# Joining the first two of three attention groups early, and the third to them last, in a two-layer encoder

## The chip, the cores and the metric

The kernel runs on one core of a Trainium2 chip. The metric is device time in microseconds (us) of one execution; the kernel before takes 2418.27 us (median of 3 runs, 2415.06 to 2419.82).

## The reference

The program is a two-layer encoder over one sequence of 1024 tokens with 1024 features, all in float32. Layer 1 mixes tokens by windowed grouped-query attention, layer 2 by dilated attention; each is followed by a SwiGLU feed-forward. Layer 2 is the one changed. It runs three attention groups (8 query heads each, heads of 64) whose outputs are combined by a softmax over the groups' log-denominators:

```python
outs, lses = [], []
for gi, (window, dil) in enumerate(((128, 1), (512, 4), (2048, 16))):
    half = window // (2 * dil)
    o, lse = banded_attention(to_strided(q[:, :, gi], dil), to_strided(k[:, :, gi], dil),
                              to_strided(v[:, :, gi], dil), half, slopes[gi], dil)
    outs.append(from_strided(o, b, dil))
    lses.append(from_strided(lse, b, dil))
alpha = softmax(stack(lses), axis=0)              # over the three groups
o = einsum('nbshg,nbshgd->bshgd', alpha, stack(outs))
x = x + g1 * (o.reshape(b, s, 512) @ w_out)
h = rmsnorm(x) * (1 + sc2) + sh2
x = x + g2 * ((silu(h @ w_gate) * (h @ w_up)) @ w_ffn_out)
```

## The kernel before

**Number format.** A float32 product is made of three products in TensorE's faster float32 format, of a rounded part ("high") and a remainder ("low") of each factor: `acc3`, lines 283 to 285. So every weight and every activation is first split: a ScalarE copy gives the high part, a VectorE or GpSimd subtraction the low part (weights: L179 on ScalarE, L180 on GpSimd; the normalised input `h` of a feed-forward: L255 on VectorE, L256 and L258 on ScalarE, L261 on VectorE or L259 on GpSimd, as the table `LOWS` says for each of 8 row blocks).

**Layer 2's attention.** `layer_b` goes through 48 *units*: 16 of group 2, then for each half `t` of the tokens 8 of group 1 and 8 of group 0. A unit has two parts. `first` makes four blocks of scores (two TensorE products each, L489 and L490), takes their maxima on VectorE (L492) and their exponentials and sums on ScalarE (L502). `second`, two units later, transposes the probabilities (L531), splits them (L533 on ScalarE, L534 on VectorE), multiplies by the values (L525) and adds two halves (L546 on ScalarE, L547 on VectorE). The outputs of groups 1 and 2 go to DRAM (`od`), as they come in another order of tokens; those of group 0 stay in SBUF (`o1`). Maxima and denominators of groups 1 and 2 take a way through DRAM as well and come back, ordered by token, by `relay(t)`: a load `rl` (L1045), a copy (L1047), four transposes (L1050) and a copy into `st12` (L1051). Units 24 to 31 are group 0 of half 0, units 40 to 47 group 0 of half 1.

**The combination of a half.** `alphas(t)` makes the weights of all three groups at once (L1066 to L1086: small VectorE operations, two ScalarE activations, four transposes L1084, the rows `al_r` L1086). `out_load` fetches the outputs of groups 1 and 2. `combine(t, g, ...)`, for each of four head pairs g, spreads the weights of the three groups over 128 partitions (three products with a 0/1 matrix `sel`, L1111), multiplies the three outputs (L1116 and L1117 with a change of the order of tokens, L1119), adds them (L1120, L1121) and splits the sum (L1122 on ScalarE, L1123 on VectorE). For half 0 this stands at units 32 to 36; for half 1 it stands behind unit 47.

**What fills TensorE beside the units.** 201 *fill* steps are handed out among the units by a table of due numbers (`FILL_B`): 160 projections of queries and keys, 32 of the output projection of half 0 (`out_0`, with residual L353 and the sums for the norm), and 9 of `up_early`, the first feed-forward tile of half 0 (8 steps of six products and an empty one). By the table 200 are handed out by unit 48; a loop behind the units hands out what is left, which is the empty one. Then `up(f)` for tiles 1 and 2 follows.

**Order.** The program is written once and a scheduler of the tile framework places each instruction in its engine's queue; each engine then works in the order of its queue. PSUM tiles are shared by tags of two buffers each: `s` (scores), `t` (transposes), `o` (outputs), and the products' banks. In `combine` the spreads take tags `o` and `s`.

Of the kernel before, what the change touches and what calls it, by code (L numbers as in the profile page):

```python
# [57 lines left out]
def f32(ap):  # L58
    return ap.bitcast(F)
# [15 lines left out]
class Trunk:  # L75
# [791 lines left out]
    def layer_b(self, h, x_src):  # L867
        nc, a, sb = self.nc, self.a, self.sb
        layer = 1
        dram = self.dram  # L870
        vd = dram.tile([T, 3, 2, P], F, name="vd")
        qd = dram.tile([3, 4, 2, P, T], F, name="qd")
# [180 lines left out]
        def alphas(t):  # L1053


            us = slice(4 * t, 4 * t + 4)

            def by_unit(ap):
                return ap.rearrange("p (u k g) -> p u k g", u=4, k=2)

            m0, l0 = (stats[0][:, :, us, s].rearrange("p k u g -> p u k g") for s in range(2))
            m, l = (st12[:, s:4:2].rearrange("p x u h -> p x (u h)") for s in range(2))
            w, e = (wk.tile([P, 3, 32], F, name=n, tag=n, bufs=1) for n in ("al_w", "al_e"))
            top = wk.tile([P, 32], F, name="al_t", tag="al_t", bufs=1)
            v = nc.vector.tensor_tensor
            v(top, m[:, 0], m[:, 1], op=ALU.min)  # L1066
            v(by_unit(top), by_unit(top), m0, op=ALU.min)
            v(by_unit(w[:, 0]), by_unit(top), m0, op=ALU.subtract)
            v(w[:, 1:3], top.unsqueeze(1).broadcast_to([P, 2, 32]), m, op=ALU.subtract)
            nc.scalar.activation(w, w, AF.Exp)  # L1070
            v(by_unit(e[:, 0]), by_unit(w[:, 0]), l0, op=ALU.mult)
            v(e[:, 1:3], w[:, 1:3], l, op=ALU.mult)
            v(top, e[:, 0], e[:, 1], op=ALU.add)
            v(top, top, e[:, 2], op=ALU.add)
            nc.vector.reciprocal(top, top)
            v(w, w, top.unsqueeze(1).broadcast_to([P, 3, 32]), op=ALU.mult)
            fl = wk.tile([P, 4, 48], R, name="al_f", tag="al_f", bufs=1)
            fv = fl.rearrange("p u (x s h) -> p x u s h", x=3, s=2)
            wv = w.rearrange("p x (u h) -> p x u h", u=4)
            nc.scalar.activation(fv[:, :, :, 0], wv, AF.Copy)  # L1080
            v(fv[:, :, :, 1], wv, f32(fv[:, :, :, 0]), op=ALU.subtract)
            tp = psp.tile([P, HT], F, name="ps_t", tag="t", bufs=2)
            for u in range(4):
                nc.tensor.transpose(tp[0:48, u * P:(u + 1) * P], f32(fl[:, u]), self.ident)  # L1084
            rows = wk.tile([48, HT], R, name="al_r", tag="al_r", bufs=1)
            nc.scalar.activation(rows, tp[0:48], AF.Copy)  # L1086
            return rows

        def out_load(t, i):

            if t == 0:
                x = self.htile([2, 2, HT], F)
                got = [x[:, 0], x[:, 1]]
            else:
                got = [wk.tile([P, 2, HT], F, name="ol", tag=tag, bufs=n) for tag, n in ((("q2", 2), ("q2", 2)), (("v", 2), ("p", 3)))[i]]
            g = slice(2 * i, 2 * i + 2)
            nc.sync.dma_start(got[0], od[1][:, g].rearrange("p g (r i) -> p g r i", r=4)[:, :, :, t * P:(t + 1) * P].rearrange("p g r i -> p (g r) i"))
            nc.sync.dma_start(got[1], od[2][:, g, t])
            return got

        def combine(t, g, got, rows):

# [3 lines left out]
            o2, o3 = (x[:, g % 2] for x in got)
            al = []
            for gi in range(3):
                ps = psp.tile([P, HT], F, name="ps_al", tag="os"[gi > 0], bufs=2)
                c = (4 * gi + g) * P  # L1110
                nc.tensor.matmul(ps, lhsT=sel[:, c:c + P], rhs=rows, start=True, stop=True)  # L1111
                al.append(ps)
            s = al[0]
            w2, w3 = (wk.tile([P, HT], F, name=n, tag="t2", bufs=self.t2) for n in ("w2", "w3"))
            v = nc.vector.tensor_tensor
            v(w2.rearrange("p (i r) -> p r i", r=4), o2.rearrange("p (r i) -> p r i", r=4), al[1].rearrange("p (i r) -> p r i", r=4), op=ALU.mult)  # L1116
            v(w3.rearrange("p (i j r) -> p j r i", j=8, r=2), o3.rearrange("p (j r i) -> p j r i", r=2, i=32),  # L1117
              al[2].rearrange("p (i j r) -> p j r i", j=8, r=2), op=ALU.mult)
            v(s, o1[t][:, g], s, op=ALU.mult)  # L1119
            v(s, s, w2, op=ALU.add)  # L1120
            v(s, s, w3, op=ALU.add)  # L1121
            nc.scalar.activation(oT[0][:, g], s, AF.Copy)  # L1122
            v(oT[1][:, g], s, f32(oT[0][:, g]), op=ALU.subtract)  # L1123
# [10 lines left out]
        def out_0(d):  # L1134
# [9 lines left out]
            self.residual(spill["x"][d], ps, layer, 2, d)  # L1144
            self.square(spill["x"][d], d, spill["ssq"], wk)
# [15 lines left out]
        for i, (gi, kv, u) in enumerate(units):  # L1161
# [44 lines left out]
        for k in range(KT):  # L1206
            nc.sync.dma_start(self.xs[0][k], spill["x"][k])
# [87 lines left out]
def _arrays(np, i):  # L1295
# [15 lines left out]
    o["sel"] = np.kron(np.eye(3), np.kron(np.ones((2, 1)), np.kron(np.eye(8).reshape(8, 2, 4).transpose(0, 2, 1).reshape(8, 8), np.ones((1, 64))))).astype(np.float32)  # L1311
# [45 lines left out]
```

## Time and profile before

| | |
|---|---|
| median of 3 runs | 2418.27 us |
| the profiled execution | 2420.43 us, its span 2418.6 us |
| TensorE (PE) busy | 2277.5 us, 94% |
| VectorE (DVE) busy | 1286.0 us, 53% |
| ScalarE (ACT) busy | 883.4 us, 37% |
| GpSimd (POOL) busy | 732.6 us, 30% |
| mean granted TensorE clock | 0.970 of 2.4 GHz |

The span is the time from the first to the last instruction of the profiled execution. Busy shares are means over stages that differ much: in the 183 us from 1480 to 1663, which hold the units from the end of half 0's group 0 to the last, TensorE is busy for 159.53, VectorE for 146.44, ScalarE for 115.62 and GpSimd for 52.14 us.

### The profile page before, as it was taken

To read this page: it belongs to the slowest core of one execution; us is meant where nothing else is said; L and a number is where in the kernel's file an instruction comes from. 1 tells how busy PE (TensorE), PEld (TensorE's weight loads), DVE (VectorE), ACT (ScalarE), POOL (GpSimd) and SP (SyncE) were. 2 spreads that over 40 slices of the span, in tenths; PEclk is the share of its full clock that TensorE was granted. 3 is DMA by queue.
4 is the path that set the end of the run, shared out by engine and by line. 5 is a ranking of instruction groups with operands and counts; after the bars stand their busy time and mean duration, and the time that the engine had idled before them with its cause. 6 is when DMAs were issued, how large, how long until landed. Compare 5 with 4: busy or idle time off the path is not lost. (4 is left out here: it accounts for less than half of the span.)

```text
span 2418.6 us, 28059 instructions
## 1 busy us (share of the span) xinstructions
PE 2277.5 (94%) x10520; PEld 1867.3 (77%) x10520; DVE 1286.0 (53%) x2263; ACT 883.4 (37%) x1754; POOL 732.6 (30%) x471
## 2 busy tenths in 40 slices
PE   6799898989999999999989999988999999999997
PEld 5587777767788888888879878665788888888886
DVE  8869999578533333333361568874633332222325
ACT  4549887232111111111252788662411111111111
POOL 4525443443122122222132344332432212221210
PEclk9899998989999999999999999987999999999998
DMA  7431123666411111111234766433221111111101
GB/s 281 157 134 36 40 92 122 217 200 220 155 60 39 49 44 53 44 53 45 82 129 156 196 188 194 152 102 111 90 79 53 44 53 53 53 50 47 53 18 70
DMA packets 128281, 242.62 MB, mean 100 GB/s; under 512 B 37632, under 2 KB 65024, under 8 KB 127120
## 3 DMA queue, kind: packets, MB, share of 16 engines
q1 hardware_dynamic: 128144, 240.82, 31.1%
q8 instruction: 83, 1.36, 0.2%
q14 instruction: 54, 0.44, 0.1%
HBM read 208.14 MB, written 30.54 MB: 99 GB/s over the span
## 5 line engine op out<-in xcount | busy, mean ns | idle before, releaser
L283 PE MATMUL ps_d<-h,w 128*128 128x512 f32 x1968 | 781.4, 399 | 16.7 <-ACT h L256 6.5
L284 PE MATMUL ps_d<-h,w 128*128 128x512 f32 x1968 | 778.2, 396 | 8.7 <-DVE h L261 7.1
L285 PE MATMUL ps_d<-h,w 128*128 128x512 f32 x1968 | 775.7, 395 | 3.5 <-POOL w L180 3.5
L180 POOL TENSOR_TENSOR w<-raw,w 128x1024 fp32r<-128x1024 f32 (+1 forms) x178 | 429.5, 2415 | 815.6 <-ACT w L179 797.9
L283 PEld LDWEIGHTS ps_d<-h,w 128*128 128x128 f32 x1968 | 375.2, 191 | 91.5 <-ACT w L179 8.6
L285 PEld LDWEIGHTS ps_d<-h,w 128*128 128x128 f32 x1968 | 375.1, 191 | 85.2 <-POOL w L180 6.0
L284 PEld LDWEIGHTS ps_d<-h,w 128*128 128x128 f32 x1968 | 376.1, 191 | 81.6 <-DVE h L261 10.2
L400 DVE TENSOR_TENSOR u<-silu,ps_d 128x512 f32<-128x512 f32 x88 | 60.4, 686 | 623.0 <-PE ps_d L285 607.1
L353 DVE SCALAR_TENSOR_TENSOR x<-ps_d,mod,x 128x512 f32<-128x512 f32 x368 | 270.3, 747 | 148.4 <-PE ps_d L285 148.2
L179 ACT ACTIVATE w<-raw 128x1024 fp32r<-128x1024 f32 (+1 forms) x178 | 185.6, 1046 | 359.6 <-PE ps_d L285 288.7
L283 PE MATMUL ps_d<-act,wo 128*128 128x512 f32 x704 | 275.9, 392 | 8.0 <-DVE x L353 4.5
L285 PE MATMUL ps_d<-act,wo 128*128 128x512 f32 x704 | 274.6, 390 | 0.0
L284 PE MATMUL ps_d<-act,wo 128*128 128x512 f32 x704 | 274.6, 390 | 0.0
L180 POOL TENSOR_TENSOR wo<-raw,wo 128x1024 fp32r<-128x1024 f32 x44 | 105.6, 2400 | 434.7 <-ACT wo L179 434.7
L179 ACT ACTIVATE wo<-raw 128x1024 fp32r<-128x1024 f32 x44 | 46.6, 1060 | 384.8 <-PE ps_d L285 340.6
L283 PEld LDWEIGHTS ps_d<-act,wo 128*128 128x128 f32 x704 | 132.5, 188 | 38.3 <-DVE x L353 6.3
L285 PEld LDWEIGHTS ps_d<-act,wo 128*128 128x128 f32 x704 | 132.5, 188 | 27.8
L284 PEld LDWEIGHTS ps_d<-act,wo 128*128 128x128 f32 x704 | 132.6, 188 | 27.0
L402 DVE TENSOR_TENSOR act<-u,act 128x512 fp32r<-128x512 f32 x88 | 126.5, 1437 | 49.0 <-ACT act L401 48.9
L152 DVE SCALAR_TENSOR_TENSOR ada_acc<-ada_w,cond,ada_acc 128x1024 f32<-128x1024 f32 x70 | 115.8, 1655 | 49.1 <-DMA ada_w<-in_ada_w 48.4
L401 ACT ACTIVATE act<-u 128x512 fp32r<-128x512 f32 x88 | 55.0, 625 | 215.1 <-DVE u L400 215.0
L534 DVE TENSOR_TENSOR pp<-ps_t,pp 128x512 fp32r<-128x512 f32 x168 | 114.9, 685 | 12.0 <-ACT pp L533 10.1
(176 smaller groups left out, 2651.9 us busy)
## 6 DMA issues: line engine op xcount, KB each, us to landing
raw<-in_ffn_w_in SPq DMA_DIRECT2D x102, 512.0 KB
ada_w<-in_ada_w SPq DMA_DIRECT2D x80, 512.0 KB
raw<-in_ffn_w_out SPq DMA_DIRECT2D x44, 512.0 KB
raw<-in_b_w_q SPq DMA_DIRECT2D x24, 512.0 KB
qd<-qo SPq DMA_DIRECT2D x48, 256.0 KB
h<-in_ada_w SPq DMA_DIRECT2D x8, 1024.0 KB
raw<-in_a_w_out SPq DMA_DIRECT2D x16, 512.0 KB
q<-qd SPq DMA_DIRECT2D x16, 512.0 KB
```

The lines of the kernel that those rows point to most:

```text
L152: nc.vector.scalar_tensor_tensor(acc, w, s, acc, op0=ALU.mult, op1=ALU.add)
L179: self.nc.scalar.activation(w[:, 0], raw, AF.Copy)
L180: self.nc.gpsimd.tensor_tensor(w[:, 1], raw, f32(w[:, 0]), op=ALU.subtract)
L283: mm(ps, lhsT=w[0], rhs=x[0], start=first, stop=False)
L284: mm(ps, lhsT=w[0], rhs=x[1], start=False, stop=False)
L285: mm(ps, lhsT=w[1], rhs=x[0], start=False, stop=last)
L353: self.nc.vector.scalar_tensor_tensor(x, ps, self.mod[:, layer, c * 8 + d:c * 8 + d + 1], x, op0=ALU.mult, op1=ALU.add)
L400: nc.vector.tensor_tensor(u, s, up, op=ALU.mult)
L401: nc.scalar.activation(act[:, 0, halves(t)], u, AF.Copy)
L402: nc.vector.tensor_tensor(act[:, 1, halves(t)], u, f32(act[:, 0, halves(t)]), op=ALU.subtract)
L534: nc.vector.tensor_tensor(pp[n, 1], tp[n], f32(pp[n, 0]), op=ALU.subtract)
```

## The change

The combination is split in two. `weights_12` makes a softmax over groups 1 and 2 alone and keeps their joint maximum and denominator (`ml12`); `join_12` weighs these two outputs and adds them in place (`o2`). `weights` makes a softmax over two terms, group 0 and the joint one, and `join` weighs and adds these. `weights_12` stands at units 29 (half 0) and 44 (half 1), `join_12` at units 30 and 31, and 45 and 46, for two head pairs each; `weights` and `join` stand where `alphas` and `combine` stood. `relay` of half 1 goes from unit 44 to 43, and the loads of the outputs follow it for both halves. The spreads of `join_12` take the tag `s`, which the scores use. Half 0's residual is written to DRAM (`x_mid`, 8 writes of 256 KB) when it is made, and loaded from there for the rest of the feed-forward, not copied from SBUF. The loop over the fill steps left goes behind the last join.

```diff
+        def weights_12():
+            m, l = (st12[:, s:4:2].rearrange("p x u h -> p x (u h)") for s in range(2))
+            w, e = small()
+            tt(ml12[:, 0], m[:, 0], m[:, 1], op=ALU.min)
+            tt(w, ml12[:, 0:1].broadcast_to([P, 2, 32]), m, op=ALU.subtract)
+            nc.scalar.activation(w, w, AF.Exp)
+            tt(e, w, l, op=ALU.mult)
+            tt(ml12[:, 1], e[:, 0], e[:, 1], op=ALU.add)
+            return rows_of(w)
+
+        def weights(t):
...
+            tt(by_unit(top), by_unit(ml12[:, 0]), m0, op=ALU.min)
...
+            nc.vector.reciprocal(top, top)
+            tt(w, w, top.unsqueeze(1).broadcast_to([P, 2, 32]), op=ALU.mult)
+            return rows_of(w)
...
+        def spread(x, g, rows, tag):
+            ps = psp.tile([P, HT], F, name="ps_al", tag=tag, bufs=2)
+            c = (4 * x + g) * P
+            nc.tensor.matmul(ps, lhsT=sel[:, c:c + P], rhs=rows, start=True, stop=True)
+            return ps
+
+        def join_12(g, x, rows):
+            o2, o3 = x[:, 0, g % 2], x[:, 1, g % 2]
+            a1, a2 = (spread(i, g, rows, "s") for i in range(2))
+            w2 = wk.tile([P, HT], F, name="w2", tag="t2", bufs=self.t2)
+            tt(w2.rearrange("p (i r) -> p r i", r=4), o2.rearrange("p (r i) -> p r i", r=4), a1.rearrange("p (i r) -> p r i", r=4), op=ALU.mult)
+            a3 = a2.rearrange("p (i j r) -> p j r i", j=8, r=2)
+            tt(a3, o3.rearrange("p (j r i) -> p j r i", r=2, i=32), a3, op=ALU.mult)
+            tt(o2, a2, w2, op=ALU.add)
+
+        def join(t, g, x, rows):
...
+            s, a12 = (spread(i, g, rows, "os"[i]) for i in range(2))
+            w2 = wk.tile([P, HT], F, name="w2", tag="t2", bufs=self.t2)
+            tt(w2, x[:, 0, g % 2], a12, op=ALU.mult)
+            tt(s, o1[t][:, g], s, op=ALU.mult)
+            tt(s, s, w2, op=ALU.add)
             nc.scalar.activation(oT[0][:, g], s, AF.Copy)
-            v(oT[1][:, g], s, f32(oT[0][:, g]), op=ALU.subtract)
+            tt(oT[1][:, g], s, f32(oT[0][:, g]), op=ALU.subtract)
...
             self.residual(spill["x"][d], ps, layer, 2, d)
+            nc.sync.dma_start(x_mid[d], spill["x"][d])
...
-            elif i in (28, 44):
+            elif i in (28, 43):
                 relay(i // 40)
-                if i == 28:
-                    got = [out_load(0, j) for j in range(2)]
+                got = [out_load(i // 40, j) for j in range(2)]
+            elif i in (29, 44):
+                rows = weights_12()
+            elif i in (30, 31, 45, 46):
+                for g in (0, 1) if i in (30, 45) else (2, 3):
+                    join_12(g, got[g // 2], rows)
             elif i == 32:
-                rows = alphas(0)
+                rows = weights(0)
             elif 33 <= i <= 36:
-                combine(0, i - 33, got[(i - 33) // 2], rows)
+                join(0, i - 33, got[(i - 33) // 2], rows)
                 if i == 36:
                     self.most = 1000
-        while self.fill:
-            self.fill_step()
-        rows = alphas(1)
-        got = [out_load(1, i) for i in range(2)]
+        rows = weights(1)
         while pend:
             run(second(*pend.popleft()))
         for g in range(4):
-            combine(1, g, got[g // 2], rows)
+            join(1, g, got[g // 2], rows)
+        while self.fill:
+            self.fill_step()
...
         for k in range(KT):
-            nc.sync.dma_start(self.xs[0][k], spill["x"][k])
+            nc.sync.dma_start(self.xs[0][k], x_mid[k])
```

Three places in the engines' queues. The first is TensorE's queue in half 0, at the end of unit 31 (group 0's last unit of that half; `q2` are its queries, `ps_s` its scores, `ps_d` a fill product, `ps_o` a weighing). Before:

```order
L525 MATMUL ps_o_12028<-pp_12034,v_11810 128x512
L489 MATMUL ps_s_12073<-kh_11107,q2_11960 128x256
L490 MATMUL ps_s_12073<-kl_11109,q2_11960 128x256
L283 MATMUL ps_d_12042<-h_9218,w_12043 128x512
L284 MATMUL ps_d_12042<-h_9218,w_12043 128x512
L285 MATMUL ps_d_12042<-h_9218,w_12043 128x512
L525 MATMUL ps_o_12028<-pp_12034,v_11810 128x512
L531 MATMUL ps_t_12105<-cst_66,p_11972 128x128 x4
L489 MATMUL ps_s_12115<-kh_9939,q2_12090 128x192
L490 MATMUL ps_s_12115<-kl_9941,q2_12090 128x192
```

Now, at the same place:

```order
L490 MATMUL ps_s_12105<-kl_11108,q2_11976 128x256
L283 MATMUL ps_d_12074<-h_9218,w_12075 128x512
L284 MATMUL ps_d_12074<-h_9218,w_12075 128x512
L285 MATMUL ps_d_12074<-h_9218,w_12075 128x512
L525 MATMUL ps_o_12152<-pp_12172,v_11809 128x512 x2
L1116 MATMUL ps_al_12122<-al_r_11974,sel_9285 128x512
L1116 MATMUL ps_al_12124<-al_r_11974,sel_9285 128x512
L1116 MATMUL ps_al_12130<-al_r_11974,sel_9285 128x512
L1116 MATMUL ps_al_12132<-al_r_11974,sel_9285 128x512
L489 MATMUL ps_s_12163<-kh_9938,q2_12138 128x192
L490 MATMUL ps_s_12163<-kl_9940,q2_12138 128x192
L489 MATMUL ps_s_12178<-kh_9938,q2_12138 128x192
```

Four spreads of `join_12` (`ps_al`) stand in a row between the last unit of group 0 and the first scores of the next unit, where a fill product and a transpose stood. The second place is VectorE's queue at the end of the units of half 1. Before, from the first split of unit 45's probabilities to the weights' last small operation but one:

```order
L534 TENSOR_TENSOR pp_13342<-ps_t_13337,pp_13342 128x512
L1068 TENSOR_TENSOR al_w_13387<-al_t_13389,stat0_9295 128x32
L1069 TENSOR_TENSOR al_w_13387<-al_t_13389,st12_9294 128x64
L547 TENSOR_TENSOR o1_1_9938<-ps_o_13285,os_13284 64x4x128
L534 TENSOR_TENSOR pp_13356<-ps_t_13351,pp_13356 128x512
L1071 TENSOR_TENSOR al_e_13388<-al_w_13387,stat0_9295 128x32
L1072 TENSOR_TENSOR al_e_13388<-al_w_13387,st12_9294 128x64
L1073 TENSOR_TENSOR al_t_13389<-al_e_13388 128x32
L1074 TENSOR_TENSOR al_t_13389<-al_t_13389,al_e_13388 128x32
L1075 RECIPROCAL al_t_13389<-al_t_13389 128x32
L547 TENSOR_TENSOR o1_1_9938<-ps_o_13336,os_13335 64x4x128
L1076 TENSOR_TENSOR al_w_13387<-al_w_13387,al_t_13389 128x96
```

Now, from unit 46's last maxima to the first of unit 47 (`h_13197` holds the loaded outputs of groups 1 and 2):

```order
L492 ISA stat0_9294 128x1
L492 ISA p_13367,stat0_9294<-ps_s_13394,bias_13208 128x256
L492 ISA stat0_9294 128x1
L1124 TENSOR_TENSOR w2_13412<-h_13197,ps_al_13408 128x4x128
L1126 TENSOR_TENSOR ps_al_13410<-h_13197,ps_al_13410 128x16x32
L547 TENSOR_TENSOR o1_1_9937<-ps_o_13425,os_13424 64x4x128
L1124 TENSOR_TENSOR w2_13420<-h_13197,ps_al_13416 128x4x128
L1127 TENSOR_TENSOR h_13197<-ps_al_13410,w2_13412 128x512
L1126 TENSOR_TENSOR ps_al_13418<-h_13197,ps_al_13418 128x16x32
L1127 TENSOR_TENSOR h_13197<-ps_al_13418,w2_13420 128x512
L492 ISA p_13434,stat0_9294<-ps_s_13436,bias_13202 128x192
L492 ISA stat0_9294 128x1
```

The weights of all groups stood there; now it is the second half of `join_12`, and unit 47's maxima are queued behind it. The third place is ScalarE's queue where the feed-forward begins. Before (`h_13467` is the combined output, `w_13595` the second weight of tile 1):

```order
L1122 ACTIVATE h_13467<-ps_al_13484 128x512
L398 ACT_TABLE_LOAD
L398 ACTIVATE silu_13576<-ps_d_12997 128x512
L1122 ACTIVATE h_13467<-ps_al_13499 128x512
L179 ACTIVATE w_13595<-raw_13596 128x1024
L401 ACTIVATE act_13575<-u_13578 128x512
L1122 ACTIVATE h_13467<-ps_al_13514 128x512
```

Now (`w_13654` is that weight):

```order
L1139 ACTIVATE h_13546<-ps_al_13558 128x512
L398 ACT_TABLE_LOAD
L398 ACTIVATE silu_13635<-ps_d_13031 128x512
L1139 ACTIVATE h_13546<-ps_al_13568 128x512
L401 ACTIVATE act_13634<-u_13637 128x512
L1139 ACTIVATE h_13546<-ps_al_13578 128x512
L179 ACTIVATE w_13654<-raw_13655 128x1024
```

The copy of the second weight stood ahead of the fourth head pair's split (L1122); now it stands behind the fourth (L1139).

## Rows read from the trace of the kernel before

**Rows 1.** Engines by stretch: busy us, instructions, TensorE clock; columns in the first line.

```profile
core 0: us, PE busy (x) PEld busy (x) DVE busy (x) ACT busy (x) POOL busy (x), PEclk, DMA share, GB/s
1480.00:1515.00 35.00, 32.20 (x183) 25.84 (x181) 28.88 (x83) 28.85 (x78) 11.89 (x10) 1.00 0.67 222
1515.00:1548.00 33.00, 30.60 (x141) 21.34 (x140) 31.52 (x67) 20.49 (x51) 10.83 (x12) 0.95 0.50 157
...
1606.00:1615.00 9.00, 9.00 (x44) 7.31 (x42) 1.12 (x4) 3.47 (x10) 2.57 (x2) 0.87 0.25 66
1615.00:1628.40 13.40, 9.26 (x52) 6.74 (x51) 10.79 (x36) 10.30 (x29) 2.71 (x2) 1.00 0.60 173
1628.40:1642.80 14.40, 13.05 (x34) 7.24 (x34) 6.89 (x9) 4.16 (x7) 0.00 (x0) 0.51 0.15 59
1642.80:1658.30 15.50, 7.57 (x12) 3.07 (x12) 15.25 (x22) 5.75 (x8) 2.35 (x1) 0.50 0.23 87
1658.30:1663.00 4.70, 4.70 (x11) 3.72 (x12) 1.07 (x2) 0.00 (x0) 0.00 (x0) 0.51 0.85 267
```

**Rows 2.** Timeline by engine: start, us, operation, [idle before it <-what ended it].

```profile
1589.39 1.08 PE L243 MATMUL ps_d<-cst,st 128*128 128x128 f32 x8
...
1603.19 2.52 POOL L259 TENSOR_TENSOR h<-ht,h 128x512 fp32r<-128x512 f32 x2 [7.67 <-ACT ht L258]
...
1609.21 1.28 POOL L259 TENSOR_TENSOR h<-ht,h 128x512 fp32r<-128x512 f32 x1 [0.93 <-ACT ht L258]
...
1614.19 0.43 PE L1050 MATMUL ps_t<-cst,rp 32*128 32x32 f32 x4
...
1614.66 0.40 ACT L1051 ACTIVATE st<-ps_t 128x128 f32<-128x128 f32 x1 [5.53 <-PE ps_t L1050]
...
1615.09 0.19 DVE L1066 TENSOR_TENSOR al_t<-st 128x32 f32<-128x32 f32 x1 [6.10 <-ACT st L1051]
```

**Rows 3.** Timeline from the weights of half 1 to the feed-forward's first tile.

```profile
1627.94 0.26 DVE L1081 TENSOR_TENSOR al_f<-al_w,al_f 128x96 fp32r<-128x96 f32 x1 [0.35 <-ACT al_f L1080]
...
1628.81 2.00 PE L531 MATMUL ps_t<-cst,p 128*128 128x128 f32 x8
...
1642.11 0.68 DVE L547 TENSOR_TENSOR o<-ps_o,os 64x512 f32<-64x512 f32 x1 [3.91 <-ACT os L546]
...
1642.83 0.69 DVE L1119 TENSOR_TENSOR ps_al<-o,ps_al 128x512 f32<-128x512 f32 x1
...
1647.28 1.70 PE L1111 MATMUL ps_al<-al_r,sel 48*128 48x512 f32 x2 [3.64 <-DVE w L1117]
...
1654.74 1.05 ACT L179 ACTIVATE w<-raw 128x1024 fp32r<-128x1024 f32 x1
...
1655.84 0.79 PE L283 MATMUL ps_d<-h,w 128*128 128x512 f32 x1 [1.73 <-ACT w L179]
...
1658.27 0.80 PE L285 MATMUL ps_d<-h,w 128*128 128x512 f32 x1 [1.22 <-POOL w L180]
```

**Rows 4.** VectorE's operations by form, 1480 to 1660 us: count, busy, mean ns, idle.

```profile
L534 DVE TENSOR_TENSOR pp<-ps_t,pp 128x512 fp32r<-128x512 f32 x45 | 30.8, 686 | 6.1 <-ACT pp L533 5.5
L492 DVE CUSTOM_DVE_ANT_0 p<-ps_s,bias 128x256 f32<-128x256 f32 x36 | 14.7, 420 | 4.0 <-PE ps_s L490 3.5 <-PE ps_t L531 0.3
...
L547 DVE TENSOR_TENSOR o<-ps_o,os 64x512 f32<-64x512 f32 x16 | 11.0, 688 | 6.8 <-ACT os L546 6.1
...
L1121 DVE TENSOR_TENSOR ps_al<-ps_al,w 128x512 f32<-128x512 f32 x8 | 5.6, 698 | 0.0
...
L1116 DVE TENSOR_TENSOR w<-ol,ps_al 128x512 f32<-128x512 f32 x4 | 4.3, 1073 | 1.3 <-PE ps_al L1111 1.3
...
L1117 DVE TENSOR_TENSOR w<-ol,ps_al 128x512 f32<-128x512 f32 x4 | 4.1, 1013 | 0.0
```

**Rows 5.** SyncE's loads near the end of the units, start and time to landing.

```profile
1605.73 0.80 SPq L1045 DMA_DIRECT2D rl<-sd  x2
...
1626.10 31.26 SPq L1207 DMA_DIRECT2D x<-h  x8
```

More of the change, by code (lines that the diff above doesn't have):

```diff
@@ L871, in layer_b @@
         vd = dram.tile([T, 3, 2, P], F, name="vd")
+        x_mid = dram.tile([KT, P, HT], F, name="x_mid_b")
         qd = dram.tile([3, 4, 2, P, T], F, name="qd")
@@ L881, in layer_b @@
         self.raw = deque([(self.main, 1), (kp, 1)])
-        sel = kp.tile([48, 12 * P], R, name="sel")
-        for i in range(3):
-            raw = kp.tile([48, HT], F, name="sel_f", tag="qo", bufs=3)
+        tt = nc.vector.tensor_tensor
+        sel = kp.tile([32, 8 * P], R, name="sel")
+        for i in range(2):
+            raw = kp.tile([32, HT], F, name="sel_f", tag="qo", bufs=3)
             nc.sync.dma_start(raw, a["sel"][:, i * HT:(i + 1) * HT])
@@ L887, in layer_b @@
         st12 = kp.tile([P, 4, 4, 8], F, name="st12")
+        ml12 = kp.tile([P, 2, 32], F, name="ml12")
         stats = [kp.tile([P, 2, 8, 2, 4], F, name=f"stat{i}") for i in range(3)]
@@ L1051, in relay @@
             nc.scalar.activation(st12.rearrange("p x u h -> p x h u"), tp.rearrange("p (x h u) -> p x h u", x=4, h=8), AF.Copy)
[L1053 to L1078, printed above, removed]
@@ L1079, in alphas, with by_unit, small, rows_of @@
+        def by_unit(ap):
+            return ap.rearrange("p (u k g) -> p u k g", u=4, k=2)
+        def small():
+            return (wk.tile([P, 2, 32], F, name=n, tag=n, bufs=1) for n in ("al_w", "al_e"))
+        def rows_of(w):
+            fl = wk.tile([P, 4, 32], R, name="al_f", tag="al_f", bufs=1)
+            fv = fl.rearrange("p u (x s h) -> p x u s h", x=2, s=2)
             wv = w.rearrange("p x (u h) -> p x u h", u=4)
             nc.scalar.activation(fv[:, :, :, 0], wv, AF.Copy)
-            v(fv[:, :, :, 1], wv, f32(fv[:, :, :, 0]), op=ALU.subtract)
+            tt(fv[:, :, :, 1], wv, f32(fv[:, :, :, 0]), op=ALU.subtract)
@@ L1101, in combine @@
-        def combine(t, g, got, rows):
+                nc.tensor.transpose(tp[0:32, u * P:(u + 1) * P], f32(fl[:, u]), self.ident)
+            rows = wk.tile([32, HT], R, name="al_r", tag="al_r", bufs=2)
+            nc.scalar.activation(rows, tp[0:32], AF.Copy)
+            return rows
+        def weights_12():
[7 more added lines that the diff above has]
+            return rows_of(w)
@@ new lines, in weights @@
+        def weights(t):
+            m0, l0 = (stats[0][:, :, 4 * t:4 * t + 4, s].rearrange("p k u g -> p u k g") for s in range(2))
+            w, e = small()
+            top = wk.tile([P, 32], F, name="al_t", tag="al_t", bufs=1)
+            tt(by_unit(top), by_unit(ml12[:, 0]), m0, op=ALU.min)
+            tt(by_unit(w[:, 0]), by_unit(top), m0, op=ALU.subtract)
+            tt(w[:, 1], top, ml12[:, 0], op=ALU.subtract)
+            nc.scalar.activation(w, w, AF.Exp)
+            tt(by_unit(e[:, 0]), by_unit(w[:, 0]), l0, op=ALU.mult)
+            tt(e[:, 1], w[:, 1], ml12[:, 1], op=ALU.mult)
+            tt(top, e[:, 0], e[:, 1], op=ALU.add)
+            nc.vector.reciprocal(top, top)
+            tt(w, w, top.unsqueeze(1).broadcast_to([P, 2, 32]), op=ALU.mult)
+            return rows_of(w)
@@ L1105, in combine @@
             oT = oTs[t]
[L1106 to L1121, printed above, removed]
+            s, a12 = (spread(i, g, rows, "os"[i]) for i in range(2))
[3 more added lines that the diff above has]
+            tt(s, s, w2, op=ALU.add)
             nc.scalar.activation(oT[0][:, g], s, AF.Copy)
-            v(oT[1][:, g], s, f32(oT[0][:, g]), op=ALU.subtract)
+            tt(oT[1][:, g], s, f32(oT[0][:, g]), op=ALU.subtract)
         wcur = {}
@@ L1310, in _arrays @@
                                  per_part(i["c"]), per_part(i["ada_b"])], axis=1))
-    o["sel"] = np.kron(np.eye(3), np.kron(np.ones((2, 1)), np.kron(np.eye(8).reshape(8, 2, 4).transpose(0, 2, 1).reshape(8, 8), np.ones((1, 64))))).astype(np.float32)
+    o["sel"] = np.kron(np.eye(2), np.kron(np.ones((2, 1)), np.kron(np.eye(8).reshape(8, 2, 4).transpose(0, 2, 1).reshape(8, 8), np.ones((1, 64))))).astype(np.float32)
     o["sink"] = c(i["a_sink"])
```

15 lines of the change are left out of this document (4 added, 11 removed).

## The prediction

> **What bounds the kernel now.** I read the windows first, then the timeline at their borders, then VectorE's operations by form. Over the whole span TensorE sets the time, but the change lies in a stretch where it does not. In the first view the reader is to compare TensorE with VectorE: from 1515 to 1548 us, where half 0 is combined, VectorE is busy for 31.52 of 33.00 us (96%), and from 1642.80 to 1658.30 for 15.25 of 15.50 us, while TensorE works for 7.57 at half its clock [rows 1]. Between these lie short stretches of the other kind: 1606 to 1615 us has TensorE without a gap and VectorE with 1.12 us of work.
>
> For half 1 the timeline gives four marks. The norm of the feed-forward's input is spread over the partitions until 1590.47 us (1589.39 + 1.08). The transposes of the relayed maxima start at A = 1614.19; VectorE idled 6.10 us for them [rows 2]. The weights of all groups are ready at X = 1627.94. The feed-forward's first tiles run without waiting from R = 1658.27, after a wait for a weight's high part (1.73 us, ScalarE's copy of 1654.74) and for its low part (1.22 us) [rows 3]. So before: 23.7 us to A, 13.75 from A to X, 30.33 from X to R. From X to 1663 us the granted clock is about 0.5, the 1.2 GHz level, after a stretch at 1.00 in which TensorE was busy for 9.26 of 13.40 us [rows 1].
>
> **The change part by part.**
>
> *The work itself.* Per half the spreads go from 12 to 16 products and the transposes of the weights from 4 to 8, which TensorE passes in under 2 us. VectorE's two reorderings per head pair stay (1.07 and 1.01 us); beside them four operations per head pair become five, so 4 operations of about 0.69 us more per half, and 3 small ones of about 0.2: 4 x 0.69 + 3 x 0.2 = 3.4 us of VectorE per half [rows 4]. In place in PSUM or not makes no difference that the rows show: 686 to 698 ns with PSUM or SBUF as output.
>
> *Half 0 (units 29 to 36).* Eight spreads with their VectorE operations move from units 33 to 36 into 30 and 31. The order shows four in a row on the scores' two buffers: the third waits until VectorE has read the first, and the next unit's scores stand behind them. In a stretch that is 96% VectorE, 3.4 us more is 3.4 us later; against it, 1480 to 1515 us leaves VectorE 6.1 us and TensorE 2.8 us idle [rows 1], which the moved operations can use. If all of it fits there: -1 (fewer operations at units 33 to 36). If TensorE stands through two head pairs' chains (2 x (1.07 + 1.01 + 0.69) = 5.5): +6. I take +2.5, near the row of 96%.
>
> *From the norm to A.* The relay stands a unit earlier, so less of the units comes ahead of it: by the order 14 score products, 5 weighings and two groups of transposes fewer, with the same 42 of 48 products of the feed-forward's first tile. At 0.12 us a score product and 0.23 a weighing (44 matmuls, two sizes, in 9.00 us [rows 1]) that is 3.5 us. The bounds are 5.5 less, as GpSimd's low parts come sooner too when ScalarE has fewer exponentials between them (it idled 7.67 us for the first [rows 2]), and 2 less, if they do not. I take -3.5. The loads from the relay took 0.80 us and started 8.5 us ahead of A [rows 5]: four loads of outputs now stand ahead of them, which are issued without waiting for an engine, so I cost these at nothing.
>
> *From A to X.* This is where the change bites. VectorE, in order, now has between st12's copy and the last unit's weights: maxima of units 45 to 47, 12 x 0.33 = 3.9 us; 8 splits of probabilities, 8 x 0.69 = 5.5; 4 sums of outputs, 2.75; `join_12`, 4 x (1.07 + 1.01 + 0.69) = 11.1; 15 small operations, 3.0; together 26.2, or about 25 as following operations overlap by some 0.07 us [rows 4]. Before, it had six splits, four sums, six maxima and the small ones. What is queued behind a `join_12` operation that waits for its spread is unit 47's maxima, and behind these the weights: each wait goes to X. With waits as from 1615 to 1628.40 (VectorE 10.79 of 13.40 us busy [rows 1]) 25 us take 31; as from 1515 to 1548 (96%) they take 26. With TensorE at 1.2 GHz its own work here (about 12 us at full clock: 32 transposes of 128, 16 weighings, 8 spreads, 20 score products, 6 of the first tile) doubles to 24, in a chain that alternates with VectorE: 37. I take 32, near the first of these rows, so +18.25 against 13.75.
>
> [...]
>
> *From X to R.* Before: weighing of the last two units among twelve spreads until the last sum of outputs at 1642.11, 14.2 us after X; then VectorE alone until the last subtractions, with TensorE waiting 3.64 us for a spread's buffer [rows 3]. Now the weighing with eight spreads, one fewer ahead of the last sum (0.43 at half clock): 13.7. Then the sum, 0.7; about 12 operations until the last head pair's add, 12 x 0.6 = 7.2 at the pitch at which such operations follow each other; waits for a spread, about 1.5; the split on ScalarE, 0.6; and behind it, as the order shows, the second weight's copy, 1.05 [rows 3]. That is 24.7, where before it was 30.3: -5.6. The bounds are 28 (the low part on GpSimd, 2.35 us as before, waits too) and 16.5 (full clock, below).
>
> *The rest.* The moved loop holds only the empty step: 0. Of the 8 writes of the residual each waits for its residual on the queue that also loads the next units' queries and values; those have been loaded units ahead, so 0, at most +1. The 8 copies of 31.26 us [rows 5] become loads from DRAM, needed only after the feed-forward's first tiles: 0. The table of `sel` is shorter: 0.
>
> *Sum.* 2.5 - 3.5 + 18.25 - 5.6 = 11.65 us on the profiled execution's 2420.43, or 2432.1. That execution is 2.16 us above the median of the runs, so 2429.9 us, which I round to 2430.
>
> **The rivals.** Less than 0.2% (4.8 us) can't be told from no change.
>
> *A. No difference.* VectorE keeps at 96% from A to X (26 us, +12.25), and half 0 costs nothing: -3.5 + 12.25 - 5.6 = +3.2, 2421.4 us. For it: it did so from 1515 to 1548 us with the same mixture of units and combinations. Against it: there TensorE had products of the fill between the spreads; from A on only six are left.
>
> *B. Faster.* The clock stays at 2.4 GHz through the last units. Before, it was at 0.51 from 1628.40 to 1663; TensorE's 13.05 us of work to 1642.80 would be 6.7 [rows 1], and with the first tile's matmuls at 0.23 in place of 0.43 us X to R falls by another 8.2, to 16.5, about what VectorE's 22 operations there take (22 x 0.69 = 15.2). With A reached 5.5 earlier, A to X at 26 and half 0 at +1: 1 - 5.5 + 12.25 - 13.8 = -6, 2412 us. It decides once A to X is below about 27 us at full clock. For it: the joins leave fewer operations behind the last unit, and six products of the first tile stand among unit 46's scores. Against it: before, the clock fell after a stretch with TensorE 69% busy [rows 1], and A to X has about 12 us of TensorE work in 32, or 38%. [...]
>
> *C. Slower still.* The clock falls to 1.2 GHz already between A and X (37 us, +5) and the four spreads in a row cost 6 in half 0 (+3.5): +20, 2438 us. For it: the 38% just named. Against it: at half clock TensorE would be busy 24 of 37 us, and VectorE's part is the same.
>
> *D. It doesn't move.* The relay or the loads come late and the joins end up behind the units anyway: then X is as before, and the 3.4 us per half are what is added, 2421 to 2425. The order speaks against it: the joins stand ahead of unit 47's maxima.
>
> **How the numbers follow.** My forecast, 2430 us, has 0.47 (its own range 2424 to 2436); C 0.18; A 0.18; B 0.13; D 0.04, half of it within 0.2%. So faster 0.13; same 0.18 and 0.02, with a little of the forecast's lower edge, 0.22; slower 0.65. The range leaves out the ends of B and C: 2414 to 2440 us.
>
> **What would show it.** Right: from A, the start of the relay's transposes, to the second weights' transposes about 32 us, VectorE over 75% busy in it with waits for spreads (`ps_al`) ahead of the reorderings; the relay 20 us after the norm; from X to the unbroken products about 25 us at a clock near 0.5; at the two units with `join_12` in half 0 waits of TensorE for VectorE that were not there. Wrong: A to X below 27 us, which means that the joins fit beside the units; a clock of 1.00 after X, which is B; or a change that sits in layer 1 or the later feed-forward, where I expect none.

## The result, and the profile after

The changed kernel takes 2430.3 us (median of 7 runs, 2422.9 to 2434.6), the kernel before 2416.2 in the same comparison: a ratio of 1.0056 (95% interval 1.0041 to 1.0071), 13.5 us slower by the ratio and 14.1 by the medians. The profiled execution took 2427.83 us, 2.5 below its median; that of before, 2420.43, lies 4.2 above its own. So the two traces differ by only 7.4 us, and 2.4 of what is missing are in layer 1, where both programs are the same: the first residual of its last step ("layer 1's end" from here on) starts at 1192.19 us before and at 1189.81 after. From that point to the end of VectorE's last operation the two traces are 9.2 us apart (9.8 by the whole times).

The windows of the changed kernel, cut at the marks of the prediction (columns as in [rows 1]):

```profile
core 0: us, PE busy (x) PEld busy (x) DVE busy (x) ACT busy (x) POOL busy (x), PEclk, DMA share, GB/s
1478.00:1513.00 35.00, 28.38 (x143) 21.07 (x143) 31.69 (x79) 23.19 (x59) 10.05 (x8) 0.94 0.58 190
1513.00:1546.00 33.00, 32.52 (x167) 24.71 (x166) 26.76 (x74) 23.88 (x64) 9.47 (x11) 0.96 0.48 159
...
1589.53:1611.48 21.95, 15.92 (x59) 11.67 (x57) 12.49 (x25) 11.99 (x26) 5.49 (x5) 0.84 0.46 142
1611.48:1640.57 29.09, 19.90 (x91) 13.16 (x90) 23.38 (x61) 15.97 (x43) 2.67 (x2) 0.85 0.13 46
1640.57:1664.35 23.78, 16.21 (x40) 8.93 (x40) 15.35 (x25) 9.97 (x15) 0.00 (x0) 0.50 0.09 30
```

And its timeline, the lines that answer to [rows 2, 3] (L1053 and L1054 are the relay's transposes and copy, L1068 and L1071 the weights' rows and their transposes):

```profile
1588.48 1.05 PE L243 MATMUL ps_d<-cst,st 128*128 128x128 f32 x8
...
1611.48 0.43 PE L1053 MATMUL ps_t<-cst,rp 32*128 32x32 f32 x4
...
1612.38 0.19 DVE L1081 TENSOR_TENSOR ml<-st 128x32 f32<-128x32 f32 x1 [6.36 <-ACT st L1054]
...
1640.57 0.23 DVE L1068 TENSOR_TENSOR al_f<-al_w,al_f 128x64 fp32r<-128x64 f32 x1 [0.32 <-ACT al_f L1067]
1640.85 1.04 PE L1071 MATMUL ps_t<-cst,al_f 128*32 128x128 f32 x4 [3.05 <-DVE al_f L1068]
...
1653.96 0.68 DVE L547 TENSOR_TENSOR o<-ps_o,os 64x512 f32<-64x512 f32 x1 [3.05 <-ACT os L546]
...
1664.35 0.80 PE L283 MATMUL ps_d<-h,w 128*128 128x512 f32 x1 [2.58 <-ACT w L179]
```

The end of each stretch less its start gives:

| stretch | before | after | difference | forecast |
|---|---|---|---|---|
| layer 1's end to half 0's norm (L225) | 390.65 | 392.36 | +1.7 | +2.5 |
| norm's sums to its spread's end | 7.63 | 7.36 | -0.3 | |
| spread's end to the relay (A) | 23.7 | 21.95 | -1.8 | -3.5 |
| A to the second weights (X) | 13.75 | 29.1 | +15.3 | +18.25 |
| X to the unbroken products (R) | 30.3 | 23.8 | -6.55 | -5.6 |

With two products more left behind R, at 0.43 us, this is the 9.2 us, to 0.1.

One trace is one execution, and other executions of the same order of instructions differ from it. The changed kernel and three of the kernels below (E1, E7, E11) have the same order up to half 0's norm: it comes 392.4, 390.9, 393.8 and 390.8 us behind layer 1's end. So one trace resolves that row to about 3 us, and its +1.7 can't be told from nothing. The spread's end to A took 21.95 us, and 22.05 and 20.15 in E1 and E11, which have the same order there. From A to the second weights' transposes E2, E3 and E11 have the change's instructions in its order (in E2 two neighbours on VectorE are swapped), and yet this stretch, 29.37 us in the change, took 33.87, 34.25 and 34.27. The change, E3 and E11:

```profile
1611.48:1640.85 29.37, 19.90 (x91) 13.16 (x90) 23.60 (x62) 15.97 (x43) 2.67 (x2) 0.85 0.13 45
```

```profile
1615.72:1649.97 34.25, 25.12 (x92) 16.93 (x91) 24.01 (x62) 16.09 (x43) 2.69 (x2) 0.68 0.12 39
```

```profile
1608.83:1643.10 34.27, 25.14 (x91) 16.98 (x91) 24.10 (x62) 16.08 (x43) 2.68 (x2) 0.67 0.12 39
```

VectorE is busy for 23.60 to 24.10 us in all three. What differs is TensorE's granted clock, 0.85 in the change's trace and 0.67 to 0.68 in the others, where TensorE needs 25.1 us for what took it 19.9. So +15.3 in the table belongs to this execution; others would have given about +20.

In half 0 the four spreads in a row are seen waiting, as the order had them:

```profile
1505.13 0.73 PE L1116 MATMUL ps_al<-al_r,sel 32*128 32x512 f32 x2
1506.80 0.49 PE L1116 MATMUL ps_al<-al_r,sel 32*128 32x512 f32 x1 [0.94 <-DVE w L1124]
1509.22 0.79 PE L1116 MATMUL ps_al<-al_r,sel 32*128 32x512 f32 x1 [1.93 <-DVE w L1124]
```

TensorE's busy time in that window falls from 32.20 of 35 us [rows 1] to 28.38, and the next window gives half of it back: 30.60 before, 32.52 now.

### The profile page after: what moved, and what is told of

It reads as the page before. It is cut to its first block, busy times and chain, and to the rows that moved or that the text cites. A ratio compares the mean times of both kernels' runs of the same rounds, so it can differ in the third digit from the quotient of the medians.

```text
span 2426.1 us, 28113 instructions
## 1 busy us (share of the span) xinstructions
PE 2277.6 (94%) x10536; PEld 1871.1 (77%) x10536; DVE 1287.2 (53%) x2277; ACT 885.9 (37%) x1759; POOL 732.4 (30%) x471
## 4 chain that ended last, share of the span: by engine, by line
PE 73%; DVE 16%; DMA 5%; issue 3%; ACT 2%; POOL 0%; SPq 0%; DVEq 0%; ACTq 0%; POOLq 0%
PE ps_d L283 22%; PE ps_d L284 22%; PE ps_d L285 22%; DMA ada_w<-in_ada_w 3%; DVE ada_acc L152 2%; DVE p L492 2%; DVE pp L534 2%; PE ps_o L525 2%; PE ps_t L531 2%; DVE p L509 1%; DVE ht L255 1%; PE ps_s L489 1%; PE ps_s L490 1%; DVE h L261 1%; DVE os L547 1%
## 5 line engine op out<-in xcount | busy, mean ns | idle before, releaser
L489 PE MATMUL ps_s<-kh,q 128*128 128x384 f32 (+3 forms) x320 | 104.4, 330 | 20.0 <-DVE ml L492 9.4
```

The lines of the kernel that those rows point to most:

```text
L489: nc.tensor.matmul(ps[:, lo:hi], lhsT=qs[g], rhs=kh, start=True, stop=False)
```

## The experiments

Each kernel ran on one chip in turn with the kernel before. E6, E8 and E10 start from the kernel before, all others from the changed kernel.

| run | median, us | ratio to before (95%) |
|---|---|---|
| E1 half 1's join_12 behind the units | 2420.9 | 1.0015 (1.0004 to 1.0026) |
| E2 half 0's join_12 late | 2433.1 | 1.0065 (1.0047 to 1.0084) |
| E3 no writes of the residual | 2434.4 | 1.0060 (1.0041 to 1.0079) |
| E4 relay in its own buffers | 2423.7 | 1.0023 (1.0013 to 1.0033) |
| E5 = E1 and E4 | 2420.0 | 1.0012 (1.0002 to 1.0023) |
| E6 kernel before, relay's own buffers | 2410.5 | 0.9976 (0.9960 to 0.9992) |
| E7 24 products held back | 2429.5 | 1.0052 (1.0037 to 1.0068) |
| E8 kernel before, 24 held back | 2418.1 | 1.0008 (0.9994 to 1.0022) |
| E9 join_12's add on GpSimd | 2421.5 | 1.0020 (1.0008 to 1.0032) |
| E10 = E6 and an add on GpSimd | 2405.9 | 0.9951 (0.9936 to 0.9966) |
| E11 last spreads four times | 2434.6 | 1.0069 (1.0056 to 1.0082) |
| E12 all joins late, own buffers | 2422.3 | 1.0019 (1.0009 to 1.0028) |

**E1.**

```diff
-            elif i in (29, 44):
+            elif i == 29:
                 rows = weights_12()
-            elif i in (30, 31, 45, 46):
+            elif i in (30, 31):
...
+        rows_12 = weights_12()
         rows = weights(1)
...
         for g in range(4):
+            join_12(g, got[g // 2], rows_12)
             join(1, g, got[g // 2], rows)
```

Expected: 

> Half 1's weights_12 and join_12 stand behind unit 47, each head pair's join_12 just ahead of its join; the rest as in the changed kernel (2430.3 us). Theory 1 (join_12 in VectorE's queue ahead of unit 47's maxima is what costs): relay to second weights falls from 29.1 us by about 12 to 17; from there to the unbroken products VectorE was idle 8.4 of 23.8 us, so 11.1 us of join_12 add 3 to 6: 27 to 30. Sum -6 to -9: 2421 to 2424 us. Rival 1 (the place doesn't matter, VectorE's work has to be done ahead of the feed-forward either way): -12 and +11, 2429 us. Rival 2 (the early place does gain): slower than 2432 us.

Measured: 2420.9 us. The windows of E1 from the norm's spread, the relay and the second weights on:

```profile
1588.17:1611.27 23.10, 16.96 (x66) 12.63 (x65) 13.44 (x30) 13.00 (x29) 6.45 (x6) 0.85 0.46 140
1611.27:1631.49 20.22, 15.33 (x86) 11.03 (x86) 16.11 (x53) 14.98 (x43) 2.64 (x2) 1.00 0.18 66
1631.49:1657.50 26.01, 19.96 (x46) 10.40 (x46) 20.77 (x32) 8.83 (x14) 0.00 (x0) 0.50 0.03 11
```

To the second weights' transposes, A to X falls from 29.4 us (34 in the other traces of the change's order) to 20.2, and X to R grows from 23.5 to 26.0. Behind the units VectorE's busy time grows by 5.6 us (15.1 to 20.8) and the stretch by 2.5 only; ahead of unit 47's maxima they cost 9 us by these traces. That is theory 1, and by the medians it is some 10 of the 13.5 us, give or take 4.5 (from the ratios, 1.0056 less 1.0015). The clock differs as well, 1.00 in E1's A to X: the gain holds what the clock makes of it.

**E2.** weights_12 of half 0 at unit 32, join_12 at units 33 to 36, each ahead of its join.

Expected: 

> Half 0's weights_12 at unit 32 and its join_12 at units 33 to 36 beside the joins; half 1 as in the changed kernel. Theory 1: half 0's early joins are 1.4 us of the change (the offset of the two traces at the norm), so 2428 to 2430 us, no measurable change. Rival: the two profiled executions hide part of it, as they differ by less (9.2 us in layer 2) than the medians (14.1): then half 0's joins cost up to 5 us more and this runs in 2424 to 2426 us.

Measured: 2433.1 us; the interval overlaps with the change's. Half 0's early place costs nothing that can be told; the rival (2424 to 2426 us) falls.

**E3.**

```diff
-            nc.sync.dma_start(x_mid[d], spill["x"][d])
...
-            nc.sync.dma_start(self.xs[0][k], x_mid[k])
+            nc.sync.dma_start(self.xs[0][k], x_src[k, :, halves(0)])
```

Expected: 

> The 8 writes of half 0's residual to DRAM are left out, and the feed-forward's residual is loaded from the layer's input instead (so that half 0's residual lacks the attention's part). Theory 1: the writes hold SyncE's queue; without them the wait of the scores for the queries (2.4 us after the norm) goes and the relay comes about 2 us sooner: 2428 us. Rival: the relay waits for the low parts of the feed-forward's input anyway, or the queries are late for another reason: 2430 us, the wait still there.

Measured: 2434.4 us. Unit 44's scores still wait 1.3 us for their queries, where the change waits 2.38, so the writes are at most part of that wait, and none of the time.

**E4.**

```diff
-            rl = wk.tile([P, HT], F, name="rl", tag="t2", bufs=self.t2)[0:32].rearrange("p (x j) -> p x j", x=4)
+            rl = wk.tile([32, HT], F, name="rl", tag="al_r", bufs=2).rearrange("p (x j) -> p x j", x=4)
```

and the same for `rp`. Expected: 

> The relay's two tiles take buffers of their own kind (those of the weights' rows) and not the three that the norm's input shares; so its load waits for no work of the norm, and in TensorE's queue its transposes stand right behind the norm's spread, ahead of the first tile's 48 products, which now stand among the joins. Theory 2 (the joins cost because the relay is late: VectorE idles 6.4 us ahead of it, and all joins fall behind it): the relay comes about 15 us sooner, VectorE's idle time is used and the products of the first tile keep TensorE busy beside the joins: second weights 8 to 12 us sooner, 2418 to 2422 us. Theory 1 alone (VectorE's queue has this much work wherever the relay stands): at most the 6.4 us of idle, 2424 us or more. A rival: the products held back beside the joins make TensorE the bound there: 2430 us.

Measured: 2423.7 us. The timeline of E4, relay and second weights:

```profile
1596.25 1.91 PE L243 MATMUL ps_d<-cst,st 128*128 128x128 f32 x8
...
1598.94 0.63 PE L1053 MATMUL ps_t<-cst,rp 32*128 32x32 f32 x4
...
1636.84 1.04 PE L1071 MATMUL ps_t<-cst,al_f 128*32 128x128 f32 x4 [3.05 <-DVE al_f L1068]
```

The relay comes 10.5 us sooner behind layer 1's end, and the second weights only 1.9 us (1636.84 - 1187.74 = 449.1, against 451.0): between them VectorE is now busy for 32.7 of 37.9 us. The gain of the medians, some 8 us, lies between the two theories, and this trace shows less of it, against a trace of the change that was fast from A to X.

**E5.** Expected: 

> Both edits: half 1's weights_12 and join_12 behind unit 47 (that alone ran in 2420.9 us), and the relay's tiles in buffers of their own (alone 2423.7). Theory (VectorE's queue between the norm and the second weights sets the end of half 1, idle time included): the 6.3 us that VectorE idles ahead of the relay go too: 2414 to 2417 us. Rival (what the early relay gained was room for the early joins, and with late joins the last unit's chain of scores, maxima and weights sets the end): 2420 to 2422 us.

Measured: 2420.0 us, the rival: with late joins the early relay brings nothing that can be told (E1 has 1.0015, E5 1.0012). The other way round, with the relay in its own buffers the late joins bring 3 us (E4 has 1.0023), less than the intervals resolve. So the two gains, 10 us in E1 and 8 in E4, are not to be added: each edit takes away nearly the same time.

**E6.** The kernel before with `rl` in the buffer of the weights' rows and `rp` in `so`, one group after the other.

Expected: 

> The kernel before, with the relay's tiles in buffers of their own (the copied tile in two parts, transposed one after the other), nothing of the change. Theory: VectorE's 6.1 us of idle time ahead of its first small operation on the relayed maxima goes, and the unit's splits that stand behind it come sooner: 4 to 6 us faster than before, 2412 to 2414 us. Rival: nothing was late behind that operation that sets the end: 2418 us.

Measured: 2410.5 us, faster than before. VectorE's waits from the norm to the weights, first of before, then of E6:

```profile
DVE al_t L1066 <- ACT st L1051: 6.1, 1, 6.1
```

```profile
DVE p L492 <- PE ps_s L490: 7.0, 7, 1.8
DVE pp L534 <- ACT pp L533: 3.2, 2, 2.7
```

The one long wait is gone, though VectorE now waits 7.0 us for scores. What the load waited for stands in the waits of SyncE's queue in the kernel before: GpSimd's low parts of the norm's input (L259), whose buffers it shares. In E6 its first half is issued at 1580.82, right behind the norm; before, both were issued from 1605.73 [rows 5].

```profile
SPq L1045 <- POOL h L259: 8.7, 1, 8.7
```

```profile
1580.82 0.34 SPq L1045 DMA_DIRECT2D rl<-sd  x1
```

The load is not all of it: before, the copy was done at 1609.0, and the transposes came at 1614.19, behind the first tile's products in TensorE's queue; in E6 and E4 the scheduler places them ahead of most of these. In this trace (layer 1's end 1188.59) the weights come 7.9 us sooner behind layer 1's end, but 5.5 of these are there at half 0's norm already, whose relay has the same buffers; and the trace is 5 us below the median of E6. So how much of the gain is the 6.1 us of half 1 is not shown.

**E7 and E8.** The table's rows `(41.5, 192), (60, 214)` become `(41.5, 192), (48, 196), (60, 214)`, and the steps left are handed out in the last two units' weighing.

Expected of E7: 

> The changed kernel with the table's last rows such that four of the first tile's eight steps (24 products) are left at unit 48, and handed out one by one between the chunks of the last two units' weighing. Theory of the clock (from the second weights to the unbroken products TensorE works at 1.2 GHz, and it is TensorE that sets the weighing there): the products keep it busy, the clock stays or comes back, that stretch falls from 23.5 to 16 to 19 us, and the relay comes 4 us sooner: 2418 to 2422 us. Rival 1: the clock stays at 1.2 GHz and 24 products of 0.43 us lengthen the stretch by up to 10, the relay comes 4 us sooner: 2430 to 2436 us. Rival 2: VectorE sets both stretches: 2426 us.

Expected of E8: 

> The same held-back products in the kernel before. Theory of the clock: from the weights to the unbroken products 27.5 us fall to 20 to 23, 2410 to 2414 us. Rival 1: at 1.2 GHz the products lengthen that stretch: 2420 to 2426 us. Rival 2: no change, 2418 us.

Measured: 2429.5 and 2418.1 us, no change in either. They did not test what they were for: the scheduler put the held-back products ahead of X all the same. E7's window from A to X:

```profile
1610.90:1643.84 32.94, 24.51 (x109) 16.43 (x109) 23.75 (x62) 16.32 (x43) 2.68 (x2) 0.91 0.12 41
```

The relay comes 3.7 us sooner behind the norm than in the change's trace, and A to X takes 3.6 us longer, with 18 more products and VectorE's busy time as ever. As the change's own order took 29.4 to 34.3 us there, this says no more.

**E9.** `join_12` writes its second product to SBUF and `nc.gpsimd.tensor_tensor(o2, w3, w2, op=ALU.add)` adds.

Expected: 

> The changed kernel, with the add of join_12 on GpSimd and not on VectorE (its factors go to SBUF). It takes 4 operations of 0.69 us from VectorE per half, adds nothing to it, and lets go of the scores' buffers one operation sooner. Theory 1 (VectorE's queue sets the time of the second weights): those come 2.5 to 5 us sooner, 2425 to 2428 us. Rival (GpSimd's add, about 1.3 us where VectorE needs 0.69, comes late for the joins): 2430 us or more.

Measured: 2421.5 us, more than expected. Relay to the second weights' transposes takes 27.0 us (1613.73 to 1640.69) against 29.4 in the change's trace; it is 7 us less than the 33.9 to 34.3 of E2, E3 and E11, near the 8.7 of the medians. Which of the two is the fair comparison stays open: E9's clock in this stretch was 0.85, as in the change's trace, and its profiled execution was the slowest of its 12 runs (2428.9), with half 0's norm 397.45 us behind layer 1's end. VectorE's two products in that stretch and GpSimd's add, E9 first, then the change:

```profile
L1124 DVE TENSOR_TENSOR w<-h,ps_al 128x512 f32<-128x512 f32 x4 | 4.3, 1077 | 0.1
L1126 DVE TENSOR_TENSOR w<-h,ps_al 128x512 f32<-128x512 f32 x4 | 4.1, 1028 | 0.0
```

```profile
L1128 POOL TENSOR_TENSOR h<-w,w 128x512 f32<-128x512 f32 x4 | 5.1, 1285 | 18.2 <-DVE w L1126 18.2
```

```profile
L1124 DVE TENSOR_TENSOR w<-h,ps_al 128x512 f32<-128x512 f32 x4 | 4.3, 1080 | 0.4 <-PE ps_al L1116 0.3
...
L1126 DVE TENSOR_TENSOR ps_al<-h,ps_al 128x512 f32<-128x512 f32 x4 | 2.9, 726 | 0.4 <-PE ps_al L1116 0.4
```

**E10.** E6, and `nc.gpsimd.tensor_tensor(w2, w2, w3, op=ALU.add)` in place of one of VectorE's adds in `combine`.

Expected: 

> The kernel before with the relay's buffers of its own (2410.5 us), and in each combination the two reordered products of groups 1 and 2 added on GpSimd while VectorE weighs group 0: VectorE has 4 operations of 0.69 us fewer per half. Theory: behind the last weighing VectorE sets the time, 2 to 3 us fewer: 2407 to 2409 us. Rival: GpSimd's add stands between the reorderings and the sum, and the two products need their buffers longer: 2410 us or more.

Measured: 2405.9 us, 0.49% faster than before and more than expected: the best of these kernels, without the change. Its interval overlaps that of E6 (0.9960 to 0.9992), so what the add gives beside the relay's buffers is just not resolved.

**E11.** In the last joins each spread is made four times into the same buffer.

Expected: 

> The changed kernel with each of the 8 spreads of half 1's last joins done four times (the same product over itself): 24 products more between the second weights and the feed-forward. If TensorE sets that stretch and stays at 1.2 GHz, 24 x 0.43 us make it up to 10 us longer: 2436 to 2440 us. If the additional work brings the clock back to 2.4 GHz, the weighing is faster, and the stretch stays as long or becomes shorter: 2424 to 2431 us. If VectorE sets it beside TensorE at 1.2 GHz: 0 to 4 us longer, 2430 to 2434 us.

Measured: 2434.6 us, by the ratios 3 us above the change. The spreads now look like this, with the clock of the stretch:

```profile
1645.86 3.78 PE L1117 MATMUL ps_al<-al_r,sel 32*128 32x512 f32 x8
...
1671.25 0.80 PE L283 MATMUL ps_d<-h,w 128*128 128x512 f32 x1
```

```profile
1640.00:1665.00 25.00, 20.38 (x53) 13.12 (x52) 9.85 (x23) 6.09 (x14) 0.00 (x0) 0.50 0.00 1
```

24 products of 0.43 us (four in a row take 2.07 us here, where the change's trace has 0.79 for one) are 10.3 us. From the second weights to the first product of the feed-forward there are 28.2 us (1643.10 to 1671.25) where the change has 19.3 (1640.85 to 1660.12): nearly all of them. The granted clock stayed at 0.50. That TensorE at this clock sets the weighing agrees with this and is not shown alone by it: each spread also stands ahead of a VectorE operation, and the scheduler changed the order, with the third and fourth spread in a row and the feed-forward's first activation behind the third split (behind the second in the change). The medians differ by 3 of these 8.9 us only, between the first and the third range expected: 2.58 are the change's wait for the second weight, which this kernel doesn't have; the other 3 are not accounted for.

**E12.** E5 with half 0 as in E2. Expected: 

> Both halves' weights_12 and join_12 late (at unit 32 and units 33 to 36, and behind unit 47), and the relay's tiles in buffers of their own: what is left of the change is the softmax in two steps (3.4 us more of VectorE per half), the writes of half 0's residual and the place of the relay. Against 2410.5 us of the kernel before with such buffers. Theory (the early place of half 0's joins takes back what its earlier relay gives, 8.4 us between the two traces at half 0's norm): 2412 to 2415 us. Rival (the two steps themselves cost it): 2418 to 2420 us, as with half 0 early (2420.0).

Measured: 2422.3 us, past the rival's range. What is left of the change (softmax in two steps, the writes, the place of the relay, the place and the buffers of the loads) costs about 10 us against E6 with no join early. These parts were not separated; in the two traces half 0's norm comes 398.0 us behind layer 1's end in E12 and 385.2 in E6, so in these two it is there by then. This bounds theory 1: with the late relay the early place of half 1's joins is 10 of the 13.5 us, but between kernels whose relays have their own buffers the change costs 11 us (E4 against E6), and the early place 3 of these (E4 against E5).

## Why the prediction was right

*The step that decides held.* "Each wait goes to X": A to X took 29.1 us, and 34 in three other traces of this order, on either side of the 32 forecast and far from before's 13.75. E1 takes 9 of the 29 away by moving `join_12` out from ahead of unit 47's maxima. In the change's trace VectorE's operations start in the order of its queue there: the second half of `join_12` from 1630.02 us to its last add at 1635.11, unit 47's first maxima at 1635.72, the second weights' rows at 1640.57. E1 agrees with it; that none of them can overtake was not tested by itself. Rival A (VectorE at 96%) fell: it was busy for 23.38 of 29.09 us, 80%, as from 1615 to 1628 before [rows 1], and for 24.1 of 34.27 in E11.

*The reason given for the waits did not.* The prediction looked for waits of VectorE for spreads ahead of the reorderings. In the change's trace those are 0.7 us of the 5.7 that VectorE is idle; the rest is spread over the relay's copy, ScalarE's splits and sums, and scores. The stretch took 29 us at a granted clock of 0.85 and 34 at 0.67 to 0.68; the prediction had a lower clock there only in its bound of 37 and in rival C.

*One price in it was too high.* VectorE's work was 23.4 us, not 25. The prediction let every reordering cost the 1.07 and 1.01 us of [rows 4] and said that in place in PSUM or not makes no difference. It does for the second: 726 ns in place, and 1028 when E9 writes it to SBUF again. Four of these are 1.2 us.

*From the norm to A is not resolved.* Of 3.5 us 1.8 came in the change's trace, 1.7 in E1's and 3.6 in E11's. The forecast had no wait in it; in the change's trace unit 44's scores stand 2.38 us for their queries:

```profile
PE ps_s L489 <- DMA q<-qd: 2.4, 1, 2.4
```

The prediction put SyncE's queue at 0 to +1, since the loads were issued units ahead; the loads here start at 1587.77 and 1588.83 us, and the scores of unit 44 could have started at about 1589.8. E3 shows that the writes are not the whole cause. On SyncE's queue the loads stand right behind the eight writes of the maxima and denominators (L1040, 1580.92 to 1587.67), in E3 too; that these hold them was not tested. The 0.80 us of [rows 5] were read as the time to landing. They are the time of the two loads on SyncE's queue: in the change the same loads start at 1603.03, and the copy that waits for them starts at 1604.80.

*From X to R held*, 23.8 us against 24.7: TensorE's wait for the second weight behind the last split (2.58 us) and the last sum 13.4 us after X (1653.96 - 1640.57; 13.7 forecast) are both there.

*Half 0* (+1.7 of +2.5 in the traces) is within the 3 us by which traces of one order differ; E2 agrees in that the early place has no measurable price.

*Rival B* fell: the clock after X was 0.50. *Rival C* came in part: from A to X the clock was 0.85 in the change's trace, where it fell some 7 us ahead of X (1.00 from 1626 to 1631 us, 0.50 from 1633.6 on), and 0.67 to 0.68 in E2, E3 and E11, with 34 us for the 37 of C. *D* fell by the order and by the trace.

*The sum* was 11.65 us; the two traces have 9.2, the ratio of the runs 13.5 and their medians 14.1. With 34.3 for 29.4 us from A to X the traces would have 14, so the change's profiled execution was probably one in which the clock held longer (0.85 there, where E2, E3 and E11 have 0.67 to 0.68). That the forecast of 2430 met the median to 0.3 us is partly luck: the difference was 2 us too small, and the kernel before was 2.1 us faster in this comparison (2416.2) than the 2418.27 that the forecast started from.

*What the prediction did not see* is that the relay itself was worth moving. It named VectorE's 6.10 us ahead of L1066 [rows 2] and took no gain from them. E6 shows that the relay's load waited for buffers that the norm's input uses, and that with buffers of its own, in both halves, the kernel before gains 0.24%.

## What to carry to other kernels

Work that was moved ahead of the end was not free here: VectorE, which it runs on, was busy for 23.38 of 29.09 us there. Ahead of such a move look first at which operations will stand behind it in the engine's queue and who waits for the last of them. What such a move costs depends on the rest of the stretch: here 10 us with a late relay and 3, not resolved, with an early one. A stretch read from one trace is one execution: the same order of instructions took 29.4 and 34.3 us. A wait of several us on one small operation is worth asking for the buffer of the load behind it: in the kernel before, a shared buffer held the relay's load for 8.7 us behind GpSimd's low parts, which have nothing to do with it. An engine next door with idle time can take an add off the busy one: here GpSimd, 30% busy, took `join_12`'s at 1.29 us for VectorE's 0.69, and the kernel ran in 2421.5 us where the change took 2430.3 (E9).

## What the runs showed of the hardware

A VectorE product of 128x512 elements with one operand read in another order took 726 ns when it went back in place to PSUM (the change), and 1013 to 1028 ns when it was written in that order to SBUF (before and E9). With TensorE busy for 20.38 of 25.00 us the granted clock stayed at 0.50 (E11, 1640 to 1665). Products of 128x512 that follow each other without a wait started 0.43 us apart at a granted clock of 0.50 (before, from 1658.87 to 1662.28) and 0.23 at 1.00 (from 1663.49 to 1670.09). The traces give the clock as a share of full speed and not in GHz: what the prediction and the expectations call 1.2 and 2.4 GHz are the granted clocks of 0.50 and 1.00 here. The same instructions from A to X, in the same order, ran at a granted clock of 0.85 in one execution (29.37 us, the change) and of 0.67 to 0.68 in two others (34.25 and 34.27 us, E3 and E11).
